# Attention pairs and output groups in a hand-written order on four engines

## The chip, the cores and the metric

The kernel runs on one core of a Trainium2 chip. The metric is the time of one execution in microseconds (us) on the device. The kernel before took 2100.49 us (median of three runs, 2097.57 to 2107.93).

The engines are named as the profile names them: PE (TensorE, with PEld for its weight loads), DVE (VectorE), ACT (ScalarE), POOL (GpSimd) and SP (SyncE, which issues the transfers). In the trace each of them runs its instructions in the order in which the program lists them, so one whose input is not there holds up what is behind it on that engine.

## The reference: what is computed

One layer of a streaming encoder for 1056 tokens (1024 of a new stream, 32 of a running one) of width 1024, all in float32:

```
x = x + 0.5 * swiglu(rmsnorm(x, g_ffn1), w1g, w1u, w1d)
mix, k, v, s = token_mixer(rmsnorm(x, g_mix), w_in, ..., w_out, sb_fn, s0, gla_chunk)
x = x + mix
x = x + 0.5 * swiglu(rmsnorm(x, g_ffn2), w2g, w2u, w2d)
return rmsnorm(x, g_final), k, v, s
```

The mixer projects its input once, and runs two groups of heads beside each other. Group A is stick-breaking attention with 8 heads of 64:

```
z = jnp.einsum('bqhd,bkhd->bhqk', q, k) * SB_SCALE
log_fail = jnp.where(causal, jax.nn.log_sigmoid(-z), 0.0)
after = lax.cumsum(log_fail, axis=3, reverse=True) - log_fail
w = jnp.where(causal, jnp.exp(jax.nn.log_sigmoid(z) + after), 0.0)
return jnp.einsum('bhqk,bkhd->bqhd', w, v)
```

Group B is gated linear attention (GLA) with 4 heads. Each head's result is normed, the GLA heads are multiplied by silu of a gate projection, and all go through one output matrix:

```
o_sb = rmsnorm(sb_fn(q_sb, k_sb, v_sb), g_sb_out)
o_g = rmsnorm(o_g, g_gla_out) * jax.nn.silu(r_g)
y = jnp.concatenate([o_sb, o_g], axis=-1) @ w_out
```

## The kernel before, in words

Tokens lie along the free dimension (1056 columns, in three pieces of 352 or four of 264), channels on the 128 partitions. Every float32 operand is kept as a high and a low half, and one product is three matmuls (`mm3`, lines 118 to 120). `split_to` makes the halves: ACT copies the high half (line 109), DVE subtracts to get the low one (line 113). For large matmuls of the two FFNs a Strassen scheme is used.

The layer runs in stages: first FFN up to about 650 us, projection and GLA to about 953 us, four **pairs** of attention heads to about 1337 us, the rest of the output projection and the second FFN to the end. The pairs are the place of the change.

**A pair.** `sb_operands` makes the halves of q and k in both halves of the partitions, and copies pieces between partition halves by DMA. A pair has 16 **blocks** (two heads, eight rows of 128 queries; `Block`). `scores` computes `z = q k` for a row on PE (lines 1572 to 1575), ACT takes two sigmoids of it, `f` of -z and `w` of z (lines 1576 and 1577), DVE runs a product scan over `f` backwards (1579) and multiplies `w` by it (1580). `turn` transposes `w` on PE, four tiles at a time, into one of two PSUM buffers `tr` (1591), and splits them into `wt`. `values` multiplies by `vs` on PE (`av`, 1604). Work of one block is spread over later ones: the list in `sb_items` puts scores of block n+3 behind the turns of block n, and the values of a block behind the turns of the next.

**Fill.** Between these items `run` lays other matmuls as fill, in proportion to weights: in pairs 0 to 2 the projection of the next pair (`pj`) and of the gates, with the norms of heads already done; in pair 3 groups of the output projection (`out_group`, `po`, 12 matmuls each) over the GLA heads. A norm (`Norm`) has statistics (`st` matmuls with ones, line 1042, of a square that ACT makes in line 1070), a root on POOL (1024), for two groups per tile a spreading of it by POOL (1077), and its application: nine transposes of the root (1096) into the same `tr` buffers and three DVE multiplies (1099).

**What sets the order.** The program emits all this in some order; in the two FFNs it stands under a manual schedule, in which each engine keeps the order of emission. In the pairs the tile scheduler reorders: it lists instructions of each engine by its own costs and by priority. SP is ordered by the scheduler in the pairs before and after the change.

**Down stage.** `Down.head` (line 880 on) is called at each product of the last gate/up step with the product's number `p`; it starts loads of parts (`part_spill`), weights (`wraw`) and of the residual `x`. `strassen` runs the down products in steps of seven. At the very end `final` norms the last 264 columns and stores eight tiles `y_out`.

Of the kernel before, what the change touches and what calls it, by code (L numbers as in the profile page):

```python
# [15 lines left out]
P = 128  # L16
D = 1024
KT = 8
# [19 lines left out]
class Slots:  # L38
# [16 lines left out]
    def run(self):  # L55
        for fn in self.at.pop(self.now, ()):
            fn()

# [785 lines left out]
class Down:  # L844
# [31 lines left out]
    def head(self, p, xd):  # L876
# [13 lines left out]
        elif p == 5:  # L890
            for d in (1, 0, 2, 3):
                self.S.nc.sync.dma_start(self.S.x[d], xd[d])
                if d == 1:
                    self.load_part(0, 6)
            self.steps[0].second(1)
# [79 lines left out]
def run(items, filler=()):  # L975
# [38 lines left out]

def rsqrt(S, st, groups):
# [12 lines left out]
def means(S, sq, ones, groups, put):  # L1028
# [5 lines left out]
    def some(b0):  # L1034
        def go():
# [7 lines left out]
            if b0 == 6:  # L1043
                put(rsqrt(S, hold["st"], groups))
# [12 lines left out]
class Norm:  # L1057
# [6 lines left out]
    def stat(self):  # L1064
# [8 lines left out]
        def put(r):  # L1073
            self.r = r
            if self.groups > 1:
                f = P // self.groups
                spread = lambda t, r: S.nc.gpsimd.tensor_copy(t.rearrange("p b (g f) -> p b g f", f=f), r.unsqueeze(3).broadcast_to([*r.shape, f]))
# [6 lines left out]
        return means(S, square, self.ones, self.groups, put)  # L1084

    def apply(self):
        S, nc, t = self.S, self.S.nc, self.t
        for b0, nb in ((0, 4), (4, 4), (NB, 1)):
            ps = S.ptr.tile([P, 4, P], F32, name="tr", tag="tr")
            rows = P if b0 < NB else DEC  # L1090
            for b in range(nb):
                if self.groups == 1:
                    r = self.r[:rows, b0 + b].broadcast_to([rows, P])
                else:
                    r = self.r[:, b0 + b] if b0 < NB else self.last[:, 0]
                nc.tensor.transpose(ps[:, b, :rows], r, S.ident[:rows, :rows])
            w = nb * P if b0 < NB else DEC
            tb = t[:, b0 * P : b0 * P + w]
            nc.vector.scalar_tensor_tensor(tb, tb, self.g, ps.rearrange("p b t -> p (b t)")[:, :w], op0=ALU.mult, op1=ALU.mult)
# [335 lines left out]
def sb_project(S, A, p, norms=()):  # L1435
# [35 lines left out]
    for n in norms[:1]:  # L1471
        spread_in(pq[0], 0, 7, n.stat())
        pq[2][8:8] = [(4, n.apply)]
    spread_in(pk[0], 2, 7, means(S, lambda: T.sq, S.ones64, 2, scales))
    for n in norms[1:]:
        spread_in(pk[1], 0, 7, n.stat())
        pv[0][4:4] = [(4, n.apply)]
# [7 lines left out]
    pv[2][0:0] = [(4, lambda: T.nk.apply())]  # L1485
# [679 lines left out]
```

## Time and profile before

| what | value |
|---|---|
| median of three runs | 2100.49 us |
| profiled execution | 2103.29 us, span 2101.5 us, granted clock 0.995 |
| busy | PE 2045.2 us (97%), DVE 1429.4 (68%), ACT 878.5 (42%), POOL 672.8 (32%) |
| pair 0 (from its first z) / 1 / 2 / 3 | 964 to 1053, to 1146, to 1244.5, to 1337 us |

The span is the stretch between the first and the last profiled instruction; 1.8 us of the execution lie around it. A row of a timeline gives start, duration, engine, source line, operation and tiles, and in brackets how long the engine stood still before it and what ended that. A matmul row's duration overlaps the next one's, so the pace is read from the starts: a 352-column matmul starts 0.16 us after the one ahead of it. PE's waits are what a change of order can move; the idle time of other engines costs nothing while PE has work.

### The profile page before, as it was taken

The page shows a single profiled execution, that of the slowest core. Times are in us where ns is not written, and L with a number is a line of the kernel's source. Part 1 is how long each engine was busy: PE and PEld are TensorE (multiplying, and loading weights), DVE is VectorE, ACT ScalarE, POOL GpSimd, SP SyncE. Part 2 cuts the span into 40 slices and gives each one's busy share as a digit, 9 for nine tenths or more (in the row PEclk, how much of TensorE's full clock was granted, in tenths as well). Part 3 has the DMA queues.
Part 4 walks back from the last instruction along what each step waited for, and adds up shares of the span by engine and source line. Part 5 has one row for each costly group of instructions (what it writes and reads, how often), then busy time and mean ns, then how long its engine had stood idle before and what let it go on. Part 6 is the DMA issues. An engine that isn't in the chain of part 4 may idle for free.

```text
span 2101.5 us, 39188 instructions
## 1 busy us (share of the span) xinstructions
PE 2045.2 (97%) x15746; PEld 1983.5 (94%) x15746; DVE 1429.4 (68%) x2225; ACT 878.5 (42%) x1623; POOL 672.8 (32%) x591
## 2 busy tenths in 40 slices
PE   7999999999999999999999999999999999999998
PEld 6999999999999988888999988899999999999997
DVE  5877777765677756377667588596776666556654
ACT  5544444441233442336555465354443333312233
POOL 0144434335773200121122101101343343367720
PEclk9999999999999999999999999999999999999999
DMA  6267677779853111203414162232673434498632
GB/s 227 103 235 259 244 247 258 260 248 383 307 211 116 53 61 61 76 34 89 119 43 118 51 187 91 97 103 77 227 258 137 154 133 154 149 383 310 228 115 69
DMA packets 140581, 350.65 MB, mean 167 GB/s; under 512 B 12904, under 2 KB 34824, under 8 KB 136816
## 3 DMA queue, kind: packets, MB, share of 16 engines
q1 hardware_dynamic: 140400, 348.16, 46.8%
q8 instruction: 124, 2.03, 0.4%
q14 instruction: 57, 0.47, 0.1%
HBM read 216.70 MB, written 124.65 MB: 162 GB/s over the span
## 4 chain that ended last, share of the span: by engine, by line
PE 85%; DVE 6%; DMA 3%; issue 2%; ACT 2%; POOL 1%; SPq 0%; DVEq 0%; ACTq 0%; POOLq 0%
PE acc_c L473 11%; PE acc_a L473 11%; PE acc_d L473 11%; PE acc_b L473 5%; PE pj L118 4%; PE pd_d L822 4%; PE pd_a L822 4%; PE pd_c L822 4%; PE acc L381 4%; PE pj L120 4%; PE pj L119 4%; PE pd L118 2%; PE pd L119 2%; PE pd L120 2%; PE pd_b L822 2%
## 5 line engine op out<-in xcount | busy, mean ns | idle before, releaser
L473 PE MATMUL acc_d<-part,S 128*128 128x264 f32 x1920 | 247.7, 285 | 0.0
L473 PE MATMUL acc_a<-h,whl 128*128 128x264 f32 x1920 | 247.4, 285 | 0.2 <-DVE whl L51 0.2
L473 PEld LDWEIGHTS acc_a<-h,whl 128*128 128x128 f32 x1920 | 239.6, 188 | 0.4 <-DVE whl L51 0.4
L473 PEld LDWEIGHTS acc_d<-part,S 128*128 128x128 f32 x1920 | 239.8, 188 | 0.1
L118 PE MATMUL pj<-h,whl 128*128 128x352 f32 x576 | 204.8, 355 | 0.0
L120 PE MATMUL pj<-h,whl 128*128 128x352 f32 x576 | 189.3, 329 | 0.0
L119 PE MATMUL pj<-h,whl 128*128 128x352 f32 x576 | 188.8, 328 | 0.0
L51 DVE TENSOR_TENSOR x<-x 128x528 fp32r<-128x528 f32 (+1 forms) x188 | 155.9, 845 | 19.1 <-ACT x L50 19.0
L50 ACT ACTIVATE x<-x 128x528 fp32r<-128x528 f32 (+1 forms) x188 | 117.3, 634 | 121.8 <-DVE x L546 37.0
L526 POOL TENSOR_TENSOR x<-tc,x 128x528 f32<-128x528 f32 x60 | 100.4, 1673 | 186.1 <-DVE tc L525 148.7
L473 PE MATMUL acc_c<-h,A 128*128 128x264 f32 x960 | 123.7, 285 | 0.6 <-DVE u L492 0.6
L473 PE MATMUL acc_c<-part,S 128*128 128x264 f32 x960 | 124.1, 285 | 0.0
L473 PE MATMUL acc_b<-h,S 128*128 128x264 f32 x960 | 123.6, 285 | 0.0
L473 PEld LDWEIGHTS acc_c<-h,A 128*128 128x128 f32 x960 | 119.7, 188 | 0.8 <-issue 0.8
L473 PEld LDWEIGHTS acc_c<-part,S 128*128 128x128 f32 x960 | 120.0, 188 | 0.0
L473 PEld LDWEIGHTS acc_b<-h,S 128*128 128x128 f32 x960 | 119.8, 188 | 0.0
L118 PEld LDWEIGHTS pj<-h,whl 128*128 128x128 f32 x576 | 109.8, 191 | 6.2 <-issue 2.5
L51 DVE TENSOR_TENSOR S<-s,S 128x512 fp32r<-128x512 f32 x152 | 114.1, 751 | 0.6 <-ACT S L50 0.6
L840 POOL TENSOR_TENSOR x<-x,u 128x528 f32<-128x528 f32 x64 | 98.3, 1555 | 45.9 <-DVE x L811 45.9
L444 POOL TENSOR_TENSOR s<-wraw 128x512 f32<-128x512 f32 x38 | 60.8, 1600 | 163.1 <-DVE S L113 97.6
L50 ACT ACTIVATE S<-s 128x512 fp32r<-128x512 f32 x152 | 93.5, 623 | 42.5 <-POOL s L447 18.6
L119 PEld LDWEIGHTS pj<-h,whl 128*128 128x128 f32 x576 | 109.9, 191 | 1.0 <-issue 0.3
(381 smaller groups left out, 4875.6 us busy)
## 6 DMA issues: line engine op xcount, KB each, us to landing
part_spill<-x SPq DMA_DIRECT2D x112, 528.0 KB, 3.8
h<-part_spill SPq DMA_DIRECT2D x64, 528.0 KB, 10.7
part<-part_spill SPq DMA_DIRECT2D x48, 528.0 KB, 10.8
win_split<-x SPq DMA_DIRECT2D x44, 512.0 KB, 3.4
whl<-win_split SPq DMA_DIRECT2D x22, 1024.0 KB, 5.0
wraw<-w1g SPq DMA_DIRECT2D x22, 512.0 KB, 5.1
wraw<-w1u SPq DMA_DIRECT2D x22, 512.0 KB, 6.4
x<-win SPq DMA_DIRECT2D x44, 256.0 KB, 3.0
```

What stands on the lines that cost most here:

```text
L50: self.later(k, lambda: nc.scalar.activation(hi, src, AF.Copy))
L51: self.later(k + 1, lambda: nc.vector.tensor_sub(lo, src, hi.bitcast(F32)))
L118: nc.tensor.matmul(out, w[:, 0, wsl], a[:, 0, asl], start=first, stop=False)
L119: nc.tensor.matmul(out, w[:, 0, wsl], a[:, 1, asl], start=False, stop=False)
L120: nc.tensor.matmul(out, w[:, 1, wsl], a[:, 0, asl], start=False, stop=last)
L381: nc.tensor.matmul(out, self.w[i](k, a), quarter(S, k, b, j), start=k == 0 and n == 0, stop=k == KT - 1 and n == 2)
L444: eng.tensor_add(self.s1, a21, a22)
L473: nc.tensor.matmul(t[:, s, :SW], w[:, a, ks], m(k, b, s), start=fresh and k == 0 and n == 0, stop=k == 3 and n == 2, skip_group_check=not ...
L526: nc.gpsimd.tensor_mul(two(hid), t, sg)
L822: nc.tensor.matmul(t[:, s, :SW], w[:, u, k * P : k * P + P], b[:, v, ss(s)], start=fresh and k == 0 and i == 0, stop=k == 1 and i == 2, sk ...
L840: nc.gpsimd.tensor_add(x[r][h], x[r][h], u)
```

## The change

Four things are changed.

1. The four pairs stand under a manual schedule for PE, DVE, ACT and POOL, so that the order of emission is the order of execution. For it the emission is rewritten: `Block.scores` emits the scan first, and its second sigmoid and product one item later (`Line`); the next pair's operands are made in four steps behind the last four turns of a pair; the norm is applied in three parts.
2. In pair 3 the groups go in the order (6,7), (4), (5), (0,1,2), with single pieces of the norms and splits between them. The last norm takes its root by ACT's reciprocal square root and a Newton step on DVE, is spread by ACT, and its result is split in three pieces of columns on ACT and DVE in place of one on ACT and POOL.
3. In both down stages the loads of the residual and of one weight tile are issued at other products.
4. Of the last eight stores, every second is issued by ACT.

```diff
+class Line:
+
+
+    def __init__(self):
+        self.q, self.now = [], 0
+
+    def __call__(self, fn):
+        self.q.append((self.now, fn))
+
+    def step(self, all=False):
+        while self.q and (all or self.q[0][0] < self.now):
+            self.q.pop(0)[1]()
+        self.now += 1
...
         elif p == 5:
-            for d in (1, 0, 2, 3):
+            self.S.nc.sync.dma_start(self.S.x[1], xd[1])
+            self.load_part(0, 6)
+            self.S.nc.sync.dma_start(self.S.x[0], xd[0])
+            self.steps[0].second(1)
+        elif p == 3:
+            self.load_step(2)
+            for d in (2, 3):
                 self.S.nc.sync.dma_start(self.S.x[d], xd[d])
...
-        for d in range(4, KT):
-            S.nc.sync.dma_start(S.x[d], xd[d])
...
                     if n == 0:
-                        self.load_step(i + 2)
+                        if i:
+                            self.load_step(i + 2)
+                    if i < 2 and n in (1, 3):
+                        d = 4 + 2 * i + n // 2
+                        S.nc.sync.dma_start(S.x[d], xd[d])
...
+        if line is not None:
+            line.step()
+    if line is not None:
+        line.step(True)
...
+    r = S.tmp.tile([P, NB + 1, groups], F32, name="nr", tag="nr", bufs=4)
+    y = r.rearrange("p b g -> p (b g)")
+    t = S.tmp.tile([P, n], F32, name="rn", tag="rn")
+    nc.scalar.activation(y, v, AF.Abs_reciprocal_sqrt, bias=S.eps)
+    nc.vector.tensor_mul(t, y, y)
+    newton(S, t, y, v)
+    return r
...
+                if now:
+                    spread = lambda t, r: S.nc.scalar.activation(*wide(t, r), AF.Copy, scale=-0.5)
...
+    def later_q():
+        tiles()
...
+    def later_k():
         a, b = T.ks
         nc.scalar.activation(a, k, AF.Copy)
         nc.sync.dma_start(b[HS[0]].bitcast(F32), a[HS[1]].bitcast(F32))
...
+    def last_k():
+        a, b = T.ks
         nc.vector.tensor_sub(a[HS[1]], k[HS[0]], a[HS[0]].bitcast(F32))
...
+    steps = [later_q, later_k, last_k, cached] if p else [both, cached]
+    return steps, rows_of(S, lambda: v, put_rows)
...
-            nc.scalar.activation(w[:, s0 : s0 + n], z[:, :n], AF.Sigmoid, scale=T.rq[:, i, h : h + 1])
+            zs.append((s0, z))
         fr = f[:, 0:L][:, ::-1]
         nc.vector.tensor_tensor_scan(fr, fr, fr, 1.0, op0=ALU.mult, op1=ALU.bypass)
-        nc.vector.tensor_mul(w[:, :L], w[:, :L], f[:, 1 : L + 1])
+
+        def rest():
+            for s0, z in zs:
+                nc.scalar.activation(w[:, s0 : s0 + n], z[:, :n], AF.Sigmoid, scale=T.rq[:, i, h : h + 1])
+            nc.vector.tensor_mul(w[:, :L], w[:, :L], f[:, 1 : L + 1])
+
+        S.line(rest)
...
             items.append((w, lambda b=b, k0=k0: b.turn(k0)))
+            if n + 2 >= len(blocks) and steps:
+                items.append((0, steps.pop(0)))
+        if n == 3:
+            items.append((1, sm.scores))
...
-                vt = sb_operands(S, A, T, 0)
+                steps, vt = sb_operands(S, A, T, 0)
+                emit(steps)
+                S.line = Line()
...
+                E = mybir.EngineType
+                eg.enter_context(tc.manual_schedule(engines={E.PE, E.DVE, E.Activation, E.Pool}))
...
-                        fill = [(12, lambda d=d, c=c: out_group(S, [(slab_a, 4)], d, c)) for ds in ((6, 7), (4, 5), (0, 1, 2)) for c in range(NCH) for d in ds]
-                        last_groups = fill[-5:]
-                        fill = fill[:-5]
-                        spread_in(fill, 1, 1, prev.stat())
-                        fill.insert(8, (4, turned))
-                        for n in range(9):
-                            fill.insert(9 + 2 * n, (1, lambda n=n: ready(n // 3, n % 3)))
-                    items = sb_items(S, A, T, p, vt)
-                    run(items, fill)
+                            nc.sync.dma_start(S.x[k], xs[k])
+
+                        order = [(d, c) for ds in ((6, 7), (4,), (5,), (0, 1, 2)) for c in range(NCH) for d in ds]
+                        groups = [(12, lambda d=d, c=c: out_group(S, [(slab_a, 4)], d, c)) for d, c in order]
+                        last_groups = groups[-5:]
+                        st, tn = prev.stat(), prev.apply()
+                        rd = [(1, lambda n=n: ready(n // 3, n % 3)) for n in range(9)]
+                        among = [st[:1], st[1:2], st[2:] + [(0, lambda: back(4))]] + [[r] for r in rd[:3]]
+                        among += [tn[:1], tn[1:2], tn[2:] + [(0, lambda: back(5))], rd[3:4], rd[4:6]] + [[r] for r in rd[6:]]
+                        fill = [x for n, g in enumerate(groups[:-5]) for x in [g] + (among[n] if n < len(among) else [])]
...
+                    run(items, fill, S.line)
                     prev = Norm(S, S.x[p], S.ones64, 2, S.vec[:, 2:3])
                     if p < 3:
-                        T = Tn
-                        vt = sb_operands(S, A, T, p + 1)
-                last_groups[0][1]()
-                for st, group in zip(prev.stat(), last_groups[1:]):
-                    st[1]()
-                    group[1]()
-                last_groups[4][1]()
-                prev.apply()
-                split_to(S, S.h[3][:, 0], S.h[3][:, 1], S.x[3], True)
+                        T, vt = Tn, hold["v"]
+                st, g = prev.stat(True), last_groups
+                for item in (g[0], st[0], g[1], st[1], st[2], g[2], g[3], g[4]):
+                    item[1]()
+                for item, n in zip(prev.apply(), (slice(0, 512), slice(512, SEQ), slice(SEQ, NR))):
+                    item[1]()
+                    split_to(S, S.h[3][:, 0, n], S.h[3][:, 1, n], S.x[3][:, n])
...
-                    nc.sync.dma_start(A["y"][d][:, ss(j)], t)
+                    (nc.scalar if last and d % 2 else nc.sync).dma_start(A["y"][d][:, ss(j)], t)
```

The emission of the first items and the manual schedule fix the start of pair 0. These are PE's rows around its first `z` (line, operation, tiles, and the queues that it waits for; `DMAHW` is a transfer). Before, there are 57 rows between the last projection matmul `pj` of pair 0 and this place, nearly all of them `pj` of pair 1:

```order
L120 MATMUL pj<-h_88,whl 128x352
L1121 MATMUL tr<-consts,vf 32x128 [waits DVE_49]
L118 MATMUL pj<-h_89,whl 128x352
L1572 MATMUL z<-ks,qh 128x128 [waits DMAHW0_49,Activation_49]
L1572 MATMUL z<-ks,qh 128x256
L119 MATMUL pj<-h_89,whl 128x352
L120 MATMUL pj<-h_89,whl 128x352
L118 MATMUL pj<-h_82,whl 128x352 [waits DVE_49]
```

Now, with the last two `pj` rows of pair 0 on top:

```order
L134 MATMUL pj<-h_89,whl 128x352
L135 MATMUL pj<-h_89,whl 128x352
L1633 MATMUL z<-ks,qh 128x128 [waits DMAHW0_49,DVE_49]
L1634 MATMUL z<-ks,ql 128x128 [waits DMAHW1_49]
L1636 LDWEIGHTS identb
L1636 MATMUL z<-maskb,identb 128x128
L1083 MATMUL st<-ones_68,x 128x1 [waits Activation_49]
L1083 MATMUL st<-ones_68,x 128x1 x2
L133 MATMUL pj<-h_82,whl 128x352 [waits DMAHW2_49]
```

The `z` of block 0 moved from behind those rows to right behind pair 0's own projection, with its second product (`ql`) and three `st` ahead of the next `pj`.

At the end of a pair, DVE's rows from the last turn of block 14 (`wt` of three tiles) to the last of block 15, which make the low halves and the next pair's `ks`; before, at the end of pair 0:

```order
L113 TENSOR_TENSOR wt<-tr,wt 128x3x128 [waits Activation_49]
L1551 TENSOR_TENSOR x<-avt,av 64x256 [waits Activation_49]
L1897 TENSOR_TENSOR rs<-rs,pj 128x352 [waits Activation_49]
L1898 TENSOR_TENSOR x<-x,rs 128x352 [waits DVE_49]
L113 TENSOR_TENSOR wt<-tr,wt 128x4x128 [waits Activation_49] x2
L1510 TENSOR_TENSOR ks<-kf,ks 64x1056 [waits DMAHW2_49]
L1551 TENSOR_TENSOR x<-avt,av 64x256 [waits Activation_49]
```

Now:

```order
L128 TENSOR_TENSOR wt<-tr,wt 128x3x128 [waits Activation_49]
L1561 TENSOR_TENSOR ks<-kf,ks 64x1056 [waits Activation_49]
L1611 TENSOR_TENSOR x<-avt,av 64x256 [waits Activation_49]
L1967 TENSOR_TENSOR rs<-rs,pj 128x352 [waits Activation_49]
L1968 TENSOR_TENSOR x<-x,rs 128x352 [waits DVE_49]
L128 TENSOR_TENSOR wt<-tr,wt 128x4x128 [waits Activation_49]
L1565 TENSOR_TENSOR ks<-kf,ks 64x1056 [waits DMAHW0_49]
L128 TENSOR_TENSOR wt<-tr,wt 128x4x128 [waits Activation_49]
L128 TENSOR_TENSOR kc<-ck,kc 64x128 [waits DMAHW4_49,Activation_49]
```

Both subtractions of `ks` moved in between the `wt` rows, and the last `wt` (line 128) now stands behind the one that waits for a DMA.

Inside a pair, DVE around the scan (`f<-f`) of a row of 768, before:

```order
L1579 SCALAR_TENSOR_TENSOR f<-f 128x768
L1580 TENSOR_TENSOR w<-w,f 128x768
L1635 SCALAR_TENSOR_TENSOR fs<-fs 32x160
L113 TENSOR_TENSOR kc<-ck,kc 64x128
L1635 SCALAR_TENSOR_TENSOR fs<-fs 32x160
L1636 TENSOR_TENSOR ws<-ws,fs 32x320
L113 TENSOR_TENSOR wt<-tr,wt 128x4x128
L113 TENSOR_TENSOR kc<-ck,kc 64x128
```

Now:

```order
L1640 SCALAR_TENSOR_TENSOR f<-f 128x768
L128 TENSOR_TENSOR wt<-tr,wt 128x4x128
L1645 TENSOR_TENSOR w<-w,f 128x768
L1702 SCALAR_TENSOR_TENSOR fs<-fs 32x160 x2
L1703 TENSOR_TENSOR ws<-ws,fs 32x320
L1640 SCALAR_TENSOR_TENSOR f<-f 128x896
L128 TENSOR_TENSOR wt<-tr,wt 128x4x128
L1507 TENSOR_SCALAR x<-pj,vec 128x352
```

The low half `wt` of an earlier block moved ahead of the product `w<-w,f`, directly behind the scan.

More of the change, by code (lines that the diff above doesn't have):

```diff
@@ L969, in plain, with run @@
                     after(c - 1)
-def run(items, filler=()):
+def run(items, filler=(), line=None):
     total, cost = sum(w for w, _ in items), sum(c for c, _ in filler)
@@ L1025, in rsqrt, with means @@
     return r
-def means(S, sq, ones, groups, put):
+def means(S, sq, ones, groups, put, root=None):
     nc = S.nc
@@ L1043, in go @@
             if b0 == 6:
-                put(rsqrt(S, hold["st"], groups))
+                put((root or rsqrt)(S, hold["st"], groups))
         return 2, go
```

97 lines of the change are left out of this document (55 added, 42 removed).

## The prediction

> **What bounds the kernel now.** I read the page first, then a table of stages by time window, then the waits of TensorE in each stage, and last the timelines at the places that the change touches.
>
> ```profile
> PE 2045.2 (97%) x15746; PEld 1983.5 (94%) x15746; DVE 1429.4 (68%) x2225; ACT 878.5 (42%) x1623; POOL 672.8 (32%) x591
> ```
>
> TensorE (PE) is busy for 97% of the span. The change leaves the number of matmuls alone, so it can only move the time in which TensorE stands still or runs at a lower clock. This is the table of stages (window, length, then busy time of PE, PEld, DVE, ACT, POOL, and the granted clock): ten microseconds ahead of the first scores, then pairs 0, 1, 2 and 3.
>
> ```profile
> 954.20:964.40 10.20, 10.20 (x74) 10.07 (x73) 7.66 (x10) 6.71 (x11) 0.00 (x0) 1.00 0.91 245
> 964.40:1053.20 88.80, 85.49 (x593) 78.78 (x592) 65.04 (x104) 53.33 (x116) 13.05 (x28) 1.00 0.30 87
> 1053.20:1146.00 92.80, 90.03 (x628) 84.02 (x628) 67.06 (x106) 50.91 (x110) 18.98 (x30) 1.00 0.30 90
> 1146.00:1244.50 98.50, 95.25 (x631) 89.53 (x630) 69.20 (x114) 54.64 (x120) 15.84 (x26) 0.97 0.32 97
> 1244.50:1337.00 92.50, 84.14 (x561) 76.76 (x560) 68.81 (x116) 48.92 (x104) 12.50 (x20) 0.96 0.25 86
> ```
>
> Length less busy time is 3.3, 2.8, 3.3 and 8.4 us for the four pairs. So the scheduler's order wastes little in pairs 0 to 2, and that is all a better order can win there. Pair 3 and the start of the output stage hold more; these are its waits (engine and line, what it waited for, us in total, times, longest), pair 3 first, then 1337 to 1410 us:
>
> ```profile
> PE tr L1096 <- POOL x L1077: 3.2, 1, 3.2
> PE tr L1591 <- DVE wt L113: 1.4, 3, 0.6
> PE po L120 <- DVE whl L113: 1.0, 1, 1.0
> PE tr L1096 <- POOL nR L1077: 0.7, 1, 0.7
> PE st L1042 <- ACT x L1070: 0.6, 1, 0.6
> PE tr L1096 <- DVE x L1099: 0.6, 1, 0.6
> PE tr L1591 <- DVE vs L113: 0.5, 1, 0.5
> PE tr L1643 <- DVE wt L113: 0.4, 1, 0.4
> ...
> PE po L118 <- ACT whl L109: 1.5, 1, 1.5
> PE po L120 <- DVE whl L113: 1.5, 2, 1.0
> PE po L118 <- DVE x L1983: 0.6, 1, 0.6
> ```
>
> **Start of pair 0.** The fixed region opens with the scores of block 0, so the first `z` now stands right behind the last projection matmul and nothing else may pass. Before, the window up to 964.4 was filled with matmuls of pair 1's projection. What `z` needs comes over SP's queue: rows of PE, SP and ACT, and the table of transfers from 954 to 972 us (median us to landing at the end).
>
> ```profile
> 954.32 0.33 PE L120 MATMUL pj<-h,whl 128*128 128x352 f32 x1
> ...
> 954.19 0.33 SPq L63 DMA_DIRECT2D whl<-win_split  x1
> ...
> 956.94 0.50 SPq L1517 DMA_DIRECT2D ql<-ql  x1
> ...
> ql<-ql SPq DMA_DIRECT2D x2, 264.0 KB, 7.7
> ...
> 952.88 1.08 ACT L1070 ACTIVATE x<-x 128x1056 f32<-128x1056 f32 x1
> ...
> 966.11 1.28 ACT L1576 ACT_TABLE_LOAD   x1 [0.52 <-PE z L1575]
> 967.41 0.37 ACT L1576 ACTIVATE f<-z,rn 128x128 f32<-128x128 f32 x1
> ```
>
> The copy of `ql` is issued at 956.94 and lands 7.7 us later, at 964.7; SP's order up to it is unchanged. TensorE has nothing to run from 954.5 to 964.7: 10.2 us. Then the three `st` matmuls of the norm are next, and their square (1.08 us, L1070's row) now stands on ACT behind the table load (1.28) and the first sigmoid (0.37): 2.7 us more. The projection work is not lost, it is only done later, so both waits are added time: 12.9 us.
>
> The clock follows. These rows are around the 3.2 us wait of pair 3; the number behind POOL's is the clock:
>
> ```profile
> 1268.00:1272.00 4.00, 0.46 (x6) 0.28 (x5) 2.33 (x5) 2.08 (x5) 3.94 (x3) 0.75 0.00 0
> 1272.00:1276.00 4.00, 4.00 (x16) 3.93 (x17) 2.88 (x3) 0.50 (x1) 0.17 (x2) 0.50 0.00 0
> 1276.00:1280.00 4.00, 4.00 (x26) 3.73 (x26) 3.64 (x10) 1.77 (x5) 0.10 (x1) 0.90 0.69 211
> ```
>
> The clock fell to 0.50 in the gap and stayed there to the end of the second row and a little beyond: short of full by 0.5 over the second row and by 0.10 over the third, 4 x 0.5 + 4 x 0.1 = 2.4 us lost. I take the same once behind the longer hole. The Trainium skill, "TensorE: Matmul & The Clock Gate", section "What's actually happening", gives the ramp as one busy window of about 3.4 us; by that figure alone this term would be an estimated 1.7 us, and the row decides. Within pair 0, the 3.3 us of old waits go; the transposes of two norms now stand in one run each, nine deep on two buffers, at about 1 us each: minus 1.3. **Pair 0: 12.9 + 2.4 - 1.3 = +14.0 us**, between +9.6 (no clock loss, all old waits gone) and +17 (clock loss, and new waits 2 us over the old).
>
> **From pair to pair.** Making the next pair's operands now starts behind the first turn of block 14 and its copies go out in a chain: split, first copies, then the copy of `ks` behind a copy that waits for the first ones, then a DVE subtraction that waits for `ks`. Behind that subtraction on DVE stands the last low half of `wt`, and TensorE's last `av` waits for it; in the old order both `wt` stood ahead. The rows, from the boundary of pairs 0 and 1 and, for transfers without a slab load (`whl`) and a store of `v` just ahead of them, from 1216 to 1245 us:
>
> ```profile
> 1027.77 1.11 SPq L1504 DMA_DIRECT2D qh<-qh  x2
> ...
> 1032.57 0.66 PE L1591 MATMUL tr<-consts,w 128*128 128x128 f32 x4 [0.45 <-DVE wt L113]
> ...
> 1033.33 0.60 ACT L109 ACTIVATE wt<-tr 128x512 fp32r<-128x512 f32 x1 [0.70 <-PE tr L1591]
> ...
> 1042.94 2.00 PE L1604 MATMUL av<-wt,vs 128*128 128x256 f32 x16
> ...
> 1042.32 0.69 DVE L113 TENSOR_TENSOR wt<-tr,wt 128x512 fp32r<-128x512 f32 x1 [1.19 <-ACT wt L109]
> 1043.04 1.25 DVE L1510 TENSOR_TENSOR ks<-kf,ks 64x1056 fp32r<-64x1056 f32 x1
> ...
> qh<-qh SPq DMA_DIRECT2D x3, 264.0 KB, 3.7
> ...
> ks<-ks SPq DMA_DIRECT2D x1, 264.0 KB, 4.5
> ```
>
> Before, the copies left at 1027.77, ahead of that turn (1032.57). Now, from the turn: transpose 0.7, `wt` 0.6, split 1.1 (as L1070), two copies 3.7 with 0.6 for the second's issue, 0.5 for the next issue, `ks` 4.5, subtraction 1.25, `wt` 0.7: 13.7 us. TensorE gets from that turn to `av` in 10.4 (1032.57 to 1042.94) and runs half of it, 1.0, without the late half: 2.3 us of wait. In pairs 1 and 2 the first `st` then stands behind `z` and waits for sigmoid and square, 0.4 + 1.1 = 1.5. **Three boundaries: 3 x 2.3 + 2 x 1.5 = +9.9.** Bounds: if the chain is ready in time only the 3.0 remains; if the copies take what they took beside a load (7.7 for 3.7) each wait is 6.3 and the sum 21.9. I take the quiet landing, since the large transfers that were beside them leave at their old place and the copies now 6 us later.
>
> **Inside pairs 1 and 2.** DVE now runs scan, low half of `wt`, product, so that a transpose buffer is read out ahead of the long product. Of 2.8 + 3.3 = 6.1 us idle I leave 4 for norms applied in one run: **-2.1**, bounds -6.1 and +2.
>
> **Pair 3.** Prior statistics, root and transposes are now pieces between groups of 12 matmuls, at 0.16 us each 1.9 us, so POOL's root and spreading (3.2 us of wait) are covered by several groups; the other waits of that stage that are not of the end add 1.4 + 0.6 + 0.5 + 0.4. They sum to 6.1, and the 2.4 us of half clock behind the long one go too. New waits for the same buffers 1.5: **-7.0**, bounds -8.5 and -2.
>
> **Last norm and output start.** The root of the last norm goes to ACT and DVE. Before, POOL took 3.2 us for it and then spread it:
>
> ```profile
> 1328.86 3.22 POOL L1024 TENSOR_TENSOR nr<-nv,mhalf 128x18 f32<-128x18 f32 x1 [28.70 <-DVE nv L1022]
> ```
>
> Now a table load (1.28), some small operations and an ACT copy of about 1 us stand under three groups of 1.9 us, so the 0.7 goes. The waits of the end and of the slabs, 1.0 + 0.7 + 0.6 + 1.5 + 0.5 + 0.6 = 4.9, shrink to the first multiply (0.6), one low half of a slab (1.0) and 0.3: **-3.0**, bounds -4.9 and 0.
>
> **Loads.** One weight load and some residual loads leave the crowded queue at the head of both down stages. What waits there now (two DVE and PE rows of the first, one of the second):
>
> ```profile
> 492.04 0.71 DVE L811 SCALAR_TENSOR_TENSOR x<-pd_d,x 128x528 f32<-128x528 f32 x1 [2.65 <-DMA x<-x]
> ...
> 493.47 0.60 PE L822 MATMUL pd_d<-part,whl 128*128 128x264 f32 x3 [1.08 <-DVE whl L51]
> ...
> 1882.42 1.73 PE L822 MATMUL pd_d<-part,whl 128*128 128x264 f32 x12 [1.42 <-DVE x L811]
> ...
> 2094.90 4.03 SPq L2061 DMA_DIRECT2D y_out<-x  x8
> ```
>
> Of the 1.08 and the 1.42 nearly all goes: **-2.5**, bounds -3.2 and +1 (the weight load itself may come late). **Last stores:** eight issues take 4.03 us on one queue; half on ACT's idle queue ends about half of it earlier: **-2.0**, bounds -2.4 and 0.
>
> Sum: 14.0 + 9.9 - 2.1 - 7.0 - 3.0 - 2.5 - 2.0 = **+7.3 us**. The profiled execution took 2103.3 us (span 2101.5 and 1.8 around it), so 2110.6 there; it was 2.8 above the median of 2100.5, so I forecast **2108 us** beside that median, 0.36% slower. What can be told from no change is 0.5%, or 10.5 us: faster means under 2090, slower over 2111.
>
> **Rivals.** (a) *Clear loss:* each boundary wait also lowers the clock and meets a load. For it: the gap of 3.2 us did so, and 2.3 us of wait plus 1.5 behind a `z` of 0.2 is nearly one such gap; against it: pair 1, with 2.8 us of idle time in several waits, kept its clock at 1.00. It decides once the wait at a boundary is as long as that 3.2 us. Price 3 x 2.4 for the clock and half the way to the 6.3 bound, 3 x 2.0: +13.2, giving 2121. The Trainium skill, same page, section "Why this matters for your kernels", allows no gaps over about 3 us; by that rule a boundary wait of 2.3 us would keep the clock and only one over about 3 would lose it; no row above has a wait between 1.5 and 3.2 us to tell.
> (b) *Clear gain:* the order holds everywhere but at the start. Pair 0 +9.6, no boundary waits, pairs 1 and 2 -6.1, pair 3 -8.5, end -4.9, loads -3.2, stores -2.4: -15.5, so 2103.3 - 15.5 - 2.8 = 2085. For it: DVE is idle for over a quarter of each pair, and reading out `wt` first is aimed at the waits that the trace has; against it: the chain of copies above is longer than TensorE's work over it.
> (c) *The hole is smaller than its rows:* `ql` lands in 3.7 instead of 7.7 us because nothing else runs: -4 us, 2104. Against it: the slab load of 954.19 still goes out 1.5 us ahead of the copies.
>
> **Numbers.** Chances: forecast 0.42 (own range 2100 to 2116), (a) 0.28, (b) 0.20, (c) 0.10. Slower takes about 0.27 of the forecast and nearly all of (a): 0.38. Faster is most of (b): 0.18. Same: 0.44. The range reaches into (b) and (a) to 2084 and 2123.
>
> **What would show it.** Right: a hole of 10 us before the first `z`, waiting for a DMA, then a wait of `st` for ACT, and a clock of 0.50 after it; `av` at the end of pairs 0 to 2 waiting for DVE `wt`; pair 3 under 4 us idle; y stores ending 2 us sooner after the last product. Wrong: no hole at 955 us, or pairs 1 and 2 shorter than before by over 3 us each, or boundary waits with the clock at half.

## The result: 4.3% slower

| | kernel before | changed kernel |
|---|---|---|
| median | 2103.95 us (4 runs) | 2194.18 us (4 runs, 2190.48 to 2194.57) |
| ratio | | 1.0431, 95% interval 1.0411 to 1.0451 |
| profiled execution | 2103.29 us, span 2101.5, clock 0.995 | 2194.41 us, span 2192.6, clock 0.970 |

The forecast was 2108, the range 2084 to 2123. The change costs about 90 us, and the forecast had 7. All ratios here are of fast executions; one of e2's ten, of 4426.95 us, is left out of its ratio. The page of the changed kernel, its busy time and the clock in 40 slices:

```profile
PE 2086.6 (95%) x15746; PEld 2018.4 (92%) x15746; DVE 1430.9 (65%) x2232; ACT 885.3 (40%) x1628; POOL 657.4 (30%) x586
...
PEclk9999999999999999989998998899999999999999
```

TensorE has the same 15746 matmuls. It is busy 41.4 us longer (2086.6 against 2045.2) and idle 49.7 us longer (2192.6 - 2086.6 = 106.0 against 56.3). The two make up the 91.1 us by which the span grew. So a little over half of the loss is waiting, and the rest is the same matmuls at a lower clock. The slices with a lower clock are those of the pairs, and so is this table by stage of the changed kernel (window, length, busy time of PE, PEld, DVE, ACT, POOL, granted clock): the wait ahead of pair 0, then pairs 0 to 3, each from its first `z` to that of the next one.

```profile
954.40:964.20 9.80, 0.56 (x3) 0.13 (x2) 5.88 (x7) 5.13 (x8) 0.00 (x0) 0.50 0.85 235
964.20:1071.95 107.75, 94.62 (x607) 87.09 (x608) 63.40 (x99) 52.49 (x110) 12.55 (x26) 0.93 0.23 64
1071.95:1194.60 122.65, 103.43 (x636) 95.11 (x636) 65.60 (x107) 52.53 (x111) 16.18 (x30) 0.89 0.22 66
1194.60:1314.80 120.20, 109.88 (x681) 102.64 (x681) 70.47 (x116) 57.03 (x121) 13.81 (x28) 0.90 0.29 86
1314.80:1430.00 115.20, 96.10 (x555) 87.86 (x554) 71.14 (x124) 53.03 (x113) 6.24 (x18) 0.85 0.21 73
```

Length less busy time is 9.2, 13.1, 19.2, 10.3 and 19.1 us: 71 us, where the table of before had 17.8. The clock is at 0.85 to 0.93 where it was 0.96 to 1.00. No other engine took up the time: over the whole span ACT is busier by 6.8 us and DVE by 1.5, and POOL less busy by 15.4. The waits of TensorE from 950 to 1440 us name many causes, none of them large:

```profile
PE st L1083 <- ACT x L1111: 11.5, 7, 2.8
PE av L1671 <- DVE wt L128: 10.0, 3, 4.8
PE tr L1143 <- DVE wt L128: 9.9, 6, 2.9
PE z L1633 <- DMA qh<-qh: 9.2, 1, 9.2
PE z L1633 <- ACT w L1644: 6.9, 12, 1.7
PE tr L1143 <- DVE x L1146: 3.6, 4, 2.1
PE av L1671 <- DVE x L1611: 3.1, 1, 3.1
...
PE st L1083 <- DVE nv L1063: 2.4, 1, 2.4
```

Lines 1083, 1143, 1633, 1658 and 1671 were 1042, 1096, 1572, 1591 and 1604 before. The first `z` stands where it was (964.2 us). The last norm's transposes come at 1429.7 us where they came at 1334.9: 94.8 us are lost between the two, and some 4 are won outside.

The start of pair 0 went as foretold; here is the timeline of TensorE there, then the clock by 4 us:

```profile
964.16 0.45 PE L1633 MATMUL z<-ks,qh 128*128 128x128 f32 x1 [9.24 <-DMA qh<-qh]
...
968.72 1.44 PE L1083 MATMUL st<-ones,x 128*128 128x1 f32 x6 [2.77 <-ACT x L1111]
...
968.00:972.00 4.00, 3.28 (x14) 3.22 (x15) 0.15 (x1) 0.66 (x1) 0.00 (x0) 0.50 0.02 4
972.00:976.00 4.00, 4.00 (x24) 3.94 (x24) 1.58 (x3) 1.63 (x4) 0.00 (x0) 0.77 0.00 0
```

What was not foretold is that this goes on all through the pairs. A wait of 2.4 us in pair 1, and the clock around it:

```profile
1117.41 1.41 PE L1083 MATMUL st<-ones,x 128*128 128x1 f32 x6 [2.37 <-DVE nv L1063]
...
1116.00:1120.00 4.00, 2.59 (x11) 2.62 (x12) 1.26 (x5) 0.94 (x1) 2.59 (x1) 0.65 0.00 0
1120.00:1124.00 4.00, 4.00 (x17) 3.93 (x17) 0.42 (x1) 0.37 (x2) 0.97 (x4) 0.50 0.00 0
1124.00:1128.00 4.00, 4.00 (x31) 3.95 (x31) 0.89 (x2) 0.85 (x2) 0.00 (x0) 1.00 0.01 4
```

In the row from 1120 TensorE is busy throughout and runs 17 matmuls, against 31 in the next one.

### The profile page after: what moved, and what is told of

It reads as the page before. It is cut to its first block, busy times and chain, and to the rows that moved or that the text cites. A ratio compares the mean times of both kernels' runs of the same rounds, so it can differ in the third digit from the quotient of the medians.

```text
span 2192.6 us, 39177 instructions
## 1 busy us (share of the span) xinstructions
PE 2086.6 (95%) x15746; PEld 2018.4 (92%) x15746; DVE 1430.9 (65%) x2232; ACT 885.3 (40%) x1628; POOL 657.4 (30%) x586
## 4 chain that ended last, share of the span: by engine, by line
PE 84%; DVE 6%; ACT 4%; DMA 3%; issue 1%; POOL 1%; SPq 0%; DVEq 0%; ACTq 0%; POOLq 0%
PE acc_c L488 10%; PE acc_a L488 10%; PE acc_d L488 10%; PE acc_b L488 5%; PE pd_d L837 4%; PE pd_a L837 4%; PE pd_c L837 4%; PE pj L133 4%; PE acc L396 4%; PE pj L134 3%; PE pj L135 3%; PE pd L133 2%; PE pd L134 2%; PE pd L135 2%; PE pd_b L837 2%; PE av L1671 1%
## 5 line engine op out<-in xcount | busy, mean ns | idle before, releaser
L133 PE MATMUL pj<-h,whl 128*128 128x352 f32 x576 | 212.9, 370 | 0.0
L135 PE MATMUL pj<-h,whl 128*128 128x352 f32 x576 | 193.6, 336 | 0.0
L134 PE MATMUL pj<-h,whl 128*128 128x352 f32 x576 | 193.3, 336 | 0.0
L51 DVE TENSOR_TENSOR x<-x 128x528 fp32r<-128x528 f32 (+1 forms) x188 | 156.4, 848 | 19.1 <-ACT x L50 19.1
L1065 POOL TENSOR_TENSOR nr<-nv,mhalf 128x18 f32<-128x18 f32 (+1 forms) x15 | 45.6, 3043 | 286.9 <-DVE nv L1063 265.9
L1640 DVE TENSOR_TENSOR_SCAN f<-f 128x128 f32<-128x128 f32 (+3 forms) x64 | 87.3, 1365 | 52.5 <-ACT f L1637 52.1
L133 PEld LDWEIGHTS pj<-h,whl 128*128 128x128 f32 x576 | 114.6, 199 | 6.5 <-issue 2.5
L134 PEld LDWEIGHTS pj<-h,whl 128*128 128x128 f32 x576 | 114.8, 199 | 1.0 <-issue 0.3
```

Of the source, the lines that this page charges most:

```text
L51: self.later(k + 1, lambda: nc.vector.tensor_sub(lo, src, hi.bitcast(F32)))
L133: nc.tensor.matmul(out, w[:, 0, wsl], a[:, 0, asl], start=first, stop=False)
L134: nc.tensor.matmul(out, w[:, 0, wsl], a[:, 1, asl], start=False, stop=False)
L135: nc.tensor.matmul(out, w[:, 1, wsl], a[:, 0, asl], start=False, stop=last)
L1065: nc.gpsimd.tensor_tensor(r.rearrange("p b g -> p (b g)"), v, S.mhalf[:, :n], op=ALU.pow)
L1640: nc.vector.tensor_tensor_scan(fr, fr, fr, 1.0, op0=ALU.mult, op1=ALU.bypass)
```

## The experiments

For each kernel I added up, from 945 to 1520 us, the pauses of TensorE of 0.8 us and more, and the clock that was missing (length times one minus granted clock, in windows of 1.7 us). The clock is at 0.50 in stretches of 3.4 us or a multiple, so it comes in units of 1.7 us. Part of the missing clock falls on time in which TensorE stood still (15.6 of 66.0 us over the whole span of the changed kernel), so the two columns do not add up to the loss. Each ratio is against the kernel before as it ran in the same batch, with medians of 2101.62 to 2103.95 us, so a difference of two medians below is good to a few microseconds.

| kernel | median, us | ratio, 95% interval | pauses: number, us | clock missing, us |
|---|---|---|---|---|
| before | 2103.95 | 1 | 8, 12.1 | 6.8 |
| changed kernel | 2194.18 | 1.0431 [1.0411, 1.0451] | 31, 62.1 | 56.3 |
| e1 loads and stores alone | 2098.62 | 0.9979 [0.9969, 0.9990] | 9, 13.0 | 5.1 |
| e2 order not fixed | 2100.46 | 0.9994 [0.9983, 1.0004] | 11, 15.4 | 6.8 |
| e3 second sigmoid at once | 2210.97 | 1.0516 [1.0498, 1.0533] | 33, 75.1 | 64.9 |
| e4 fill before the scores | 2186.90 | 1.0405 [1.0384, 1.0426] | 29, 52.4 | 49.5 |
| e5 operands earlier | 2182.76 | 1.0384 [1.0366, 1.0403] | 32, 59.7 | 46.1 |
| e6 norms in pieces | 2190.40 | 1.0429 [1.0401, 1.0456] | 30, 62.9 | 51.2 |
| e9 only PE fixed | 2145.34 | 1.0209 [1.0186, 1.0232] | 23, 44.8 | 25.6 |
| e10 PE not fixed | 2127.97 | 1.0126 [1.0104, 1.0148] | 14, 27.3 | 22.2 |
| e11 square ahead | 2161.34 | 1.0278 [1.0254, 1.0303] | 23, 45.9 | 35.8 |
| e12 four mends | 2147.37 | 1.0215 [1.0195, 1.0235] | 18, 31.8 | 22.2 |

### The loads and stores alone (e1)

The kernel before with only parts 3 and 4 of the change:

```diff
         elif p == 5:
-            for d in (1, 0, 2, 3):
+            self.S.nc.sync.dma_start(self.S.x[1], xd[1])
+            self.load_part(0, 6)
+            self.S.nc.sync.dma_start(self.S.x[0], xd[0])
...
-                    nc.sync.dma_start(A["y"][d][:, ss(j)], t)
+                    (nc.scalar if last and d % 2 else nc.sync).dma_start(A["y"][d][:, ss(j)], t)
```

> The kernel before with two parts of the change alone: the moved loads at the heads of the two down stages, and every second one of the last eight stores issued by ACT. In the profile of the changed kernel the first down stage (from its first matmul to the end of the FFN) is 2.8 us shorter, the second 1.7 us, the end 0.7 us. Theory (these parts gain and the pairs lose): 5 us under the kernel before, within 2 us. Rival (these stages only look shorter because the rest of the changed kernel left the queues in another state): no difference from the kernel before, within 2 us.

Measured 0.9979 [0.9969, 0.9990], which is 4.4 us of 2101.62; the medians of the same batch differ by 3.0 us. These two parts are a gain of about the size foretold. It is under the 0.5% taken as what can be told, but over ten runs the interval lies below one. This is the fastest kernel of the study, ahead of both.

### The new emission, but not fixed (e2)

```diff
-                eg.enter_context(tc.manual_schedule(engines={E.PE, E.DVE, E.Activation, E.Pool}))
```

> The changed kernel without the manual schedule over the four pairs: the same items are emitted in the same order, and the scheduler orders the engines again. Theory (the loss lies in executing the emission in order, 50 us of TensorE waits in the pairs plus 41 us of work at the half clock that follows them): 2090 to 2105 us, with under 25 us of TensorE waits from 950 us on. Rival (the loss lies in what is emitted where: operands of the next pair late, second sigmoid one item later): still over 2130 us, with waits at the ends of the pairs.

Measured 2100.46 us, ratio 0.9994 [0.9983, 1.0004]. The page has TensorE back at its old busy time:

```profile
PE 2043.8 (97%) x15746; PEld 1982.9 (95%) x15746; DVE 1431.7 (68%) x2232; ACT 881.8 (42%) x1628; POOL 663.1 (32%) x586
```

So nothing that the change computes is dear: with the scheduler free to move them, the deferred sigmoid, the steps for the next operands, the other root and the order of groups together cost about 2 us beside e1. Keeping to the emitted order costs the other 94. What each of these parts would cost in a fixed order, this run does not tell.

### The second sigmoid at once (e3)

```diff
-        S.line(rest)
+        rest()
```

> The changed kernel with the second sigmoid and the product emitted at once, not one item later. Theory (the held-back sigmoid keeps the two buffers of z occupied: waits of z and zs for ACT w 9.5 us, of tr for DVE w 2.0 us, in the changed kernel): these 11.5 us fall under 3, and with a few half-clock stretches of 1.7 us lost each the time goes to 2172 to 2182 us. Rival (holding it back is what keeps the transpose buffers free; without it wt stands behind the product on DVE): waits for DVE wt grow by as much, and the time is 2190 us or more.

Measured 2210.97 us, 17 us slower still. The suspicion was that `Line` holds buffers of `z` too long. It does: the wait of `z` for ACT's `w` fell from 6.9 to 2.1 us. But the same edit puts the long product ahead of what DVE owes TensorE:

```profile
PE tr L1143 <- DVE wt L128: 13.7, 6, 3.3
PE st L1083 <- ACT x L1111: 13.3, 8, 3.0
PE av L1671 <- DVE wt L128: 13.1, 7, 4.6
PE tr L1658 <- DVE wt L128: 9.9, 7, 3.1
```

The deferral is worth keeping once the order is fixed.

### Three single mends (e4, e5, e6)

e4 lets 19 pieces of fill run ahead of the first scores, so that TensorE has work while `qh` and `ql` are copied:

```diff
+    for _, fn in filler[:ahead]:
+        fn()
+    filler = list(filler[ahead:])
...
-                    run(items, fill, S.line)
+                    run(items, fill, S.line, 0 if p else 19)
```

> The changed kernel with 19 pieces of the fill (about 8 us of pair 1's projection matmuls, with the statistics of the norm) emitted ahead of the first scores of pair 0, the rest of the fill spread evenly. Theory (the hole before the first z and the half clock behind it cost what they show: 9.9 us of waits, 2.8 us of st waiting for ACT, and 968 to 974 us at half clock): wait for qh and ql about 2 to 4 us, the rest of pair 0 as it was: 2178 to 2186 us. Rival (the hole only takes the place of waits that come later in pair 0, where DVE and ACT set the pace): under 4 us gained, 2190 us or more.

Measured 2186.90 us, 7.3 less. The wait for `qh` is gone. Others grew (`z` behind ACT's `w` to 8.2 us, the weight slab of `po` from 1.6 to 3.1), so that TensorE's idle time fell by 6.6 us where the hole had 12.7, and only 7 came back.

e5 makes the next pair's operands one block earlier and puts the last subtraction behind the last `wt`:

```diff
-            if n + 2 >= len(blocks) and steps:
+            if (n, k0) in ((13, 0), (13, 4), (15, 4)) and steps:
                 items.append((0, steps.pop(0)))
...
+    items += [(0, fn) for fn in steps]
     items.append((1, late))
```

> The changed kernel with the next pair's operands made one block earlier (q behind the first turn of block 13, k behind its second) and the subtraction that waits for the copy of ks emitted behind the last wt of the pair. Theory (the chain of copies holds up the last wt and by it av at the three ends of pairs: 10.0 us of waits of av for DVE wt, and the half clock behind them): these waits fall under 2 us, no new wait of z over 2 us, 2176 to 2186 us. Rival (the chain is only moved on: z of the next pair waits for ks instead): under 5 us gained.

Measured 2182.76 us, 11.4 less, inside the expected range. The wait of `av` at the ends of the pairs, still above the 2 us expected:

```profile
PE av L1671 <- DVE wt L128: 3.4, 2, 3.1
```

It was 10.0 in three. The three boundaries are a real cause, with the mechanism of the prediction, but an eighth of the loss.

e6 spreads each norm's nine transposes into three pieces between fill:

```diff
-        pq[2][8:8] = [(4, lambda n=n: [x[1]() for x in n.apply()])]
+        spread_in(pq[2], 2, 2, n.apply())
...
-        pv[0][4:4] = [(4, lambda n=n: [x[1]() for x in n.apply()])]
+        spread_in(pv[0], 1, 2, n.apply())
...
```

> The changed kernel with the nine transposes of each norm in pairs 0 to 2 emitted in three pieces with two pieces of projection between them, in place of one run. Theory (nine transposes in a run on two buffers wait for wt and for the multiplies: tr for DVE wt 9.9 us, for DVE x 3.6 us in the changed kernel, 11.9 of them in pairs 0 to 2): these fall to 5 us or less, 2178 to 2187 us. Rival (the transposes wait because the buffers are taken by turns of blocks whatever stands between them): the waits keep within 3 us of what they were, 2190 us or more.

Measured 2190.40 us, 3.8 less by the medians, but the ratio (1.0429) is that of the changed kernel (1.0431), so no gain is shown; a miss. The wait of line 1143 behind `wt` fell from 9.9 to 2.3 us, but its wait for the multiply (`x`, line 1146) rose from 3.6 to 6.3, and the pauses in all stayed (62.9 us). So a wait that was taken away came back at other operands.

### What a wait costs (e7, e8)

To price a wait by itself, twenty were put into the second gate/up stage of the kernel before, where TensorE otherwise never stands still: a matmul, four ACT copies of its result one behind the other, and a matmul that needs the last copy. e8 has eleven copies.

```diff
+        if role == "b" and S.holes:
+            x = S.tmp.tile([P, P], F32R, name="hx", tag="hx", bufs=1)
+            nc.tensor.matmul(t[:, 0, :SW], w[:, 0, :P], m(0, 0, 0), start=True, stop=True)
+            for _ in range(4):
+                nc.scalar.activation(x, t[:, 0, :P], AF.Copy)
+            nc.tensor.matmul(t[:, 0, :P], w[:, 0, :P], x, start=True, stop=True)
...
```

> The kernel before with 20 holes in the second gate/up stage, one per step of about 20 us: TensorE runs one extra 264-column matmul, ACT copies 128 columns of its result four times, and TensorE waits for that with a second extra matmul. The stage has no waits and a clock of 1.00 before. It gives the price of a wait. Theory (a wait costs itself, and 3.4 us at half clock behind it, 1.7 us, as the 33 such losses beside 31 gaps of 0.8 us or more in the pairs of the changed kernel suggest): holes of 1.2 to 1.6 us, clock down behind most of them, 50 to 75 us over the kernel before. Rival (a wait of this length leaves the clock alone, as several did in the kernel before): 26 to 38 us over it, clock 1.00 in the stage.

> As the kernel with 20 holes, but eleven copies by ACT in each, for holes of about 3 us. Theory (each such wait is followed by one stretch at half clock): 20 x 3 us of waits, 5 us of extra matmuls and 20 x 1.7 us, 95 to 105 us over the kernel before. Rival (no clock loss): 62 to 70 us over it. A second rival (the clock falls for two stretches behind waits of 3 us): over 120 us.

Measured 2190.02 us (1.0411 [1.0374, 1.0449]) and 2239.24 us (1.0652 [1.0634, 1.0670]). The holes came out longer than meant. The waits of TensorE and two of the twenty holes in the first kernel:

```profile
PE acc_b L474 <- ACT hx L473: 51.9, 20, 3.2
...
1448.94 0.33 PE L474 MATMUL acc_b<-hx,S 128*128 128x128 f32 x1 [1.29 <-ACT hx L473]
1469.73 0.33 PE L474 MATMUL acc_b<-hx,S 128*128 128x128 f32 x1 [2.72 <-ACT hx L473]
```

and the same waits in the second, with the clock around its first hole (3.45 us, up to 1450.56):

```profile
PE acc_b L474 <- ACT hx L473: 95.1, 20, 5.4
...
1448.00:1452.00 4.00, 1.44 (x8) 1.44 (x9) 0.00 (x0) 2.77 (x10) 0.00 (x0) 0.87 0.00 0
1452.00:1456.00 4.00, 4.00 (x26) 4.00 (x26) 0.50 (x1) 0.00 (x0) 0.00 (x0) 0.70 0.00 0
```

In e7 the span grew by 84.3 us: 51.9 of waiting, 29.0 of missing clock (17 units of 1.7), and the added matmuls. So a hole with a wait of 2.6 us costs 4.2, its two matmuls included. In e8 it grew by 135.7: 95.1 of waiting and 39.2 of clock (23 units), 6.8 for a wait of 4.75. The clock's share grows less than the length: 17 units behind 20 waits of 2.6 us, 23 behind 20 of 4.75, all of which are charged. Behind the shorter ones it is not sure: twelve holes of e7 have the 17 units, and eight, of 1.29 to 3.08 us, have none. The Trainium skill, "TensorE: Matmul & The Clock Gate", section "What's actually happening", says that the activity window of about 3.4 us runs freely. The units of 3.4 us at half clock, and that the same hole is charged in one place and not in another, agree with that.

The trace shows what decides in e7. The starts of its twelve stretches at half clock lie whole steps of 3.413 us apart (1540.24, 1567.55, 1594.85 us and so on). Laid on these steps, a free hole leaves TensorE idle for at most 1.89 us of any one step, because the edge between two steps splits it: 2.72 us into 1.55 and 1.17, 3.08 into 1.73 and 1.35. Eleven of the twelve charged holes leave it idle for 1.98 us or more of one step, and the twelfth (3.24 us) for 1.80. These are the free hole of 3.08 us and a charged one of 2.19, cut at the edges of the steps:

```profile
1489.03:1492.45 3.42, 1.69 (x14) 1.48 (x13) 3.42 (x3) 1.56 (x3) 3.42 (x3) 1.00 0.63 249
1492.45:1495.86 3.41, 2.06 (x17) 2.06 (x18) 0.09 (x1) 2.25 (x7) 2.51 (x2) 1.00 0.73 257
...
1615.33:1618.75 3.42, 1.23 (x10) 1.02 (x9) 1.34 (x3) 2.66 (x7) 0.00 (x0) 1.00 0.71 237
1618.75:1622.16 3.41, 3.41 (x18) 3.41 (x17) 0.00 (x0) 0.00 (x0) 0.00 (x0) 0.50 0.63 228
```

In the pairs of the changed kernel the same steps tell less. Fourteen of its sixteen stretches follow a step with 1.4 to 3.4 us idle, and short waits add up there (1.12 and 1.09 us ahead of 997.7). Two, from 953.4 and 1257.1 us, follow a step with 0.31 us idle or less; why, no run separates.

### Whose order costs (e9, e10)

```diff
-                eg.enter_context(tc.manual_schedule(engines={E.PE, E.DVE, E.Activation, E.Pool}))
+                eg.enter_context(tc.manual_schedule(engines={E.PE}))
```

> The changed kernel with the fixed order kept for TensorE alone: DVE, ACT and POOL are ordered by the scheduler over the pairs, as before. Theory P (TensorE's own order, written down with no slack between an operand and its use, is what costs): the waits stay near 70 us over the stage and so does half clock, 2165 to 2195 us. Theory D (the order of DVE and ACT delivers the operands late): with those two free the waits fall to some 30 us, 2100 to 2125 us.

and with `engines={E.DVE, E.Activation, E.Pool}` instead:

> The mirror of it: DVE, ACT and POOL keep the written order over the pairs, TensorE is ordered by the scheduler. Theory P: TensorE then runs what is ready, and the stage loses little, 2100 to 2125 us. Theory D: the operands still come late whatever TensorE does with the time, 2150 to 2195 us. If both kernels come out slow, each order alone is enough to make the waits; if both come out fast, only the two together are.

Measured 2145.34 us (+43.6 over the kernel before in the same batch) and 2127.97 us (+26.2). Neither theory holds alone. With TensorE's order fixed, the scheduler moves ACT's square forward (the wait of `st` falls from 11.5 to 2.6 us) and the waits of `av` behind `wt` fall from 10.0 to 0.3 us, but the hole at the start stays:

```profile
PE z L1633 <- DMA qh<-qh: 9.2, 1, 9.2
PE tr L1143 <- DVE wt L128: 9.1, 4, 3.1
PE tr L1658 <- DVE wt L128: 7.1, 5, 2.5
...
PE st L1083 <- ACT x L1111: 2.6, 2, 1.3
```

With TensorE free and the others fixed, the hole is gone, since TensorE takes other matmuls there:

```profile
PE po L133 <- DVE x L1775: 6.0, 2, 3.5
PE tr L1143 <- DVE wt L128: 5.2, 5, 2.3
...
PE po L133 <- DMA whl<-wo_split: 3.7, 1, 3.7
PE st L1083 <- ACT x L1111: 2.5, 1, 2.5
...
PE av L1671 <- DVE wt L128: 1.3, 2, 1.0
```

TensorE's own order is the larger part. The two alone add to 70 us and together cost 90: about 20 us come only where both are fixed.

### The square one block ahead (e11) and all mends together (e12)

ACT's square of a norm stood right ahead of the three pieces that sum it. Now it is an item of its own, seven pieces of fill earlier:

```diff
-                hold["sq"] = sq()
...
-    return [some(b0) for b0 in (0, 3, 6)]
+    return [(0, lambda: hold.update(sq=sq()))] + [some(b0) for b0 in (0, 3, 6)]
...
```

The edit reaches every norm, also those ahead of pair 0 and the last one.

> The changed kernel with the square of each norm written as an item of its own, one block (7 pieces of fill) ahead of the matmuls that sum it (st). My theory: the 11.5 us of st behind ACT's square (7 places) fall below 3 us, with the half clock behind them, 2180 to 2187 us. Rival: the chain of the norm is only started earlier and waits at its next link (the transposes behind the split of wt), 2191 us or more.

Measured 2161.34 us, 32.8 less than the changed kernel: the direction of my theory and more than twice its size (7 to 14). TensorE's waits from 950 to 1450 us, with lines one lower:

```profile
PE tr L1142 <- DVE wt L128: 10.1, 7, 2.2
PE av L1670 <- DVE wt L128: 9.5, 3, 4.6
PE z L1632 <- DMA qh<-qh: 7.0, 1, 7.0
PE z L1632 <- ACT w L1643: 6.1, 11, 1.7
```

The waits of `st` (11.5 behind the square, 2.4 behind the root) are gone. Pauses fell by 16.2 us and missing clock by 20.5. The first `z` comes at 960.1 us, 4.1 sooner, so this much of the gain lies ahead of the pairs. In the changed kernel four of the seven waits of `st` for the square stand within 6 us behind another wait (the hole, two of the `av`, one for a weight slab). The second wait of such a pair goes with more missing clock: behind `av` and `st` the clock stays down for 10.2 us from 1069.4 and for 13.7 from 1188.9, and in e11, where `av` waits almost as long (2.77 and 4.58 us) and no `st` behind it, for 6.8 each.

e12 has e4, e5, e6 and e11 at once.

> The four mends together: the fill ahead of the first scores, the next block's operands one block earlier, the norm's transposes in three pieces, the squares ahead. If they add (about -7, -11, -3 and -7 to -11 us), 2160 to 2168 us. Rival: a wait that is taken away leaves TensorE earlier at the next operand that is late, so the mends share their gain, 2172 us or more. By either, the order without slack stays 55 us or more over the kernel before.

Measured 2147.37 us: 46.8 less, where the four alone give 7.3 + 11.4 + 3.8 + 32.8 = 55.3. They nearly add, and the remaining loss, 45.6 us, is smaller than the 55 I held for sure. Its list shows what is left, mostly waits of about a microsecond and a few of 4:

```profile
PE tr L1659 <- DVE wt L128: 10.2, 10, 2.0
PE z L1634 <- ACT w L1645: 8.1, 12, 1.7
PE av L1672 <- DVE wt L128: 5.3, 4, 4.3
PE tr L1169 <- DVE vs L128: 4.0, 1, 4.0
```

## Why the prediction was wrong

Worked in idle and busy time of TensorE, the error is plain: the sum foresaw +7.3 us of idle time and none of busy time (2.4 of clock lost at the start, 2.4 won in pair 3). Measured were +49.7 and +41.4.

- **Start of pair 0: right.** 9.2 + 0.7 for the copies and 2.8 behind ACT's square against 10.2 and 2.7, with the clock at 0.50 behind it. That the hole lowered the clock is not shown, for it fell at 953.4 us, 1.6 ahead of the hole. The rival of a smaller hole is out.
- **Boundaries: right mechanism, a little small.** `av` waited 2.8, 4.8 and 2.4 us against 2.3 each, the first `st` of pairs 1 and 2 waited 1.5 each as forecast: 13.0 against 9.9.
- **Inside the pairs: this failed, on the idle side.** I took 4 us for pairs 1 and 2 and 1.5 of new waits in pair 3. TensorE's waits from 950 to 1440 us sum to 71.6; without the hole (12.7) and the boundaries (13.0) some 46 are left, where the forecast's terms leave about 12. On the rows of before they were small or missing, because the scheduler had put something else in their place: `st` behind the square at four more places, the norm's transposes behind `wt` of blocks (9.9, before 4.1) and behind their own multiplies (3.6, before 0.6), `z` behind the deferred second sigmoid (6.9, before none). POOL was one too, which I had as cleared in pair 3 only: in pairs 0 to 2 its root still runs, and the one-column memset of `f` now stands behind it on POOL, with DVE's product and TensorE behind that:

```profile
1085.37 3.89 POOL L1065 TENSOR_TENSOR nr<-nv,mhalf 128x18 f32<-128x18 f32 x1 [36.03 <-DVE nv L1063]
...
1090.66 0.56 DVE L1645 TENSOR_TENSOR w<-w,f 128x384 f32<-128x384 f32 x1 [4.22 <-POOL f L1627]
...
1091.27 0.55 PE L1658 MATMUL tr<-consts,w 128*128 128x128 f32 x3 [2.04 <-DVE w L1645]
```

  I bounded this term by +2 at the worst, and for that I read old waits and not the new order: the rows of the new order had to be gone through for every operand that is made right ahead of its use.
- **The clock: this failed, on the busy side.** It was priced once, at 2.4 us, behind the longest hole. In the changed kernel 33 units of 1.7 us stand beside 31 pauses. The table of before had a sign of it: the 0.97 of pair 2 is a stretch of 6.8 us at half clock from 1191.5 us with no wait of 0.5 us near it, behind matmuls of which twelve `st` have two columns each. Rival (a) had the mechanism, that a boundary wait lowers the clock, but let it begin at a wait of 3.2 us; 2.4 us did it in the rows above, and e7 charged waits of 2.2. The rule I set beside it, of the Trainium skill, "TensorE: Matmul & The Clock Gate", section "Why this matters for your kernels", that allows gaps up to about 3 us, does not hold here.
- **Pair 3: failed in sign.** POOL's wait of 3.2 us is gone, as forecast, and sixteen others came: 19.1 us idle against 8.4, at a clock of 0.85, where the forecast left 3.8 us idle and a clock without that loss.
- **Output start: small.** It took 1.3 us less, against 3.0.
- **Loads and last stores: right in sum, wrong in the parts.** e1 has 4.4 us for both, the forecast 4.5. In the changed kernel the two down stages are 2.8 and 1.7 us shorter, against 2.5 for both, and the end after the last product is 0.7 us shorter, against 2.0. SP's queue does issue half as many stores, in 1.8 us instead of 4.0:

```profile
2186.68 1.80 SPq L2142 DMA_DIRECT2D y_out<-x  x4
```

  The last of the eight is issued 0.8 us behind the last multiply instead of 2.3, but it takes 2.4 us to land instead of 2.0, and 1.3 us follow its landing instead of 0.9: so 0.7 of the 1.5 us reach the end.

The clear gain (b) is out by e2, e9 and e10: no fixing of this order, on either side, gained anything.

## What to carry to other kernels

When an order that a scheduler found is replaced by one written down, do not carry the old list of waits over: it lists what was left after everything else had been moved out of the way. Go through the new order operand by operand, and ask for each whether its maker stands one full item ahead of its use on the maker's own queue. Price a wait of TensorE at more than its length, also when it is only two microseconds long: twenty of 2.6 us cost 84 us here, not 52, and short waits close together add up. And test the parts apart: two small moves of loads and stores were the gain of this change, keeping to the written order its loss.

## What the runs showed of the hardware

Half clock follows waits shorter than the 3.2 us that I had taken as the limit: in e7, where TensorE was otherwise fully busy, waits of 2.19 us were charged, and 17 units of 1.7 us stand behind twelve of the twenty holes. A longer wait (4.75 us) was always charged, but mostly one unit. What decides there is the idle time within one step of 3.413 us: holes with up to 1.89 us went free, those with 1.98 us or more were charged, and one with 1.80 was charged too. So holes of 2.72 and 3.08 us, the second and third of e7, went free, and some of 2.19 did not. In the pairs and in the kernel before, three stretches at half clock stand behind steps in which TensorE hardly waited (953.4 and 1257.1 us; 1191.5 us in the kernel before), so this is not the whole of it.
